# Two MLPs' first matrix: seven block products over six of eight input tiles, three tiles of h in DRAM, copies issued later

## The chip, the core and the metric

The kernel runs on one core of a Trainium2 chip. The time is device microseconds of that core for one launch; the time before is the median of three runs. The comparison asks for the same time, less or more.

## What is computed

Two groups of tokens, a prompt of 1024 and eight samples of eight, go through a trunk of two layers. Layer 0 mixes by gated linear attention, layer 1 by sliding-window attention; both have a squared-ReLU MLP from 1024 to 4096 features and back, and a per-layer input (PLE). The change touches the MLPs and what leads to them:

```python
def sq_relu_mlp(hn, w_up, w_down):
    return jnp.square(jax.nn.relu(hn @ w_up)) @ w_down
for i in range(DEPTH):                         # DEPTH = 2
    hn = rmsnorm(h, w['norm_mix'][i])
    ...                                        # y: the layer's mixer
    h = h + y
    h = h + sq_relu_mlp(rmsnorm(h, w['norm_mlp'][i]), w['w_up'][i], w['w_down'][i])
    gate = jax.nn.sigmoid(rmsnorm(h, w['norm_ple'][i]) @ w['w_ple_gate'][i])
    h = h + gate * (p[i] @ w['w_ple'][i])
```

All of it is fp32: w_up is 1024 x 4096 and w_down 4096 x 1024 in each layer.

## The kernel before

The 1088 tokens lie transposed, features on the partitions: the residual h is eight tiles of 128 x 1088 fp32, and a matmul streams token columns past a 128 x 128 block of weights. Every fp32 product is three matmuls of a narrower fp32 kind (`mm3`, L186 to L191): an operand is split into a rounded part `hi` and a rest `lo`, and hi.hi, hi.lo and lo.hi are added up in PSUM. A **k-unit** below is one input tile against one 128-wide block of weights and half of a pair's columns: two chunks of 272 columns, three matmuls each, so six matmuls.

Weights come from DRAM as fp32. SP issues the loads (`load`, L76) in one fixed order, the one in which the program asks for them; a DMA that must wait holds up those behind it on SP. `wfill` (L116 to L144) prepares weights three entries ahead of their use: a raw tile (two buffers), ScalarE's cast to `whi` (L142), VectorE's difference to `wlo` (L143), five buffers each. The order on each engine is set by a tile scheduler when the program is built and is fixed from then on.

An MLP (`mlp`, L817) has eight blocks fb of 512 hidden features. A block is two calls of `up_pair` (L741), each making two 128-wide hidden tiles, and then eight **down tiles**: for each of the eight tiles of h, 36 matmuls of 362 or 364 columns, and VectorE adds the result to h (L841). The last block begins the next norm behind each of its tiles and opens the pools of the PLE (`ple_open`, L851), whose input `praw` is loaded, cast (L218) and split (L219) there, twice, through one buffer.

`up_pair` views weights and tokens as 2 x 2 blocks. Over four of the eight input tiles (0, 1 and 2, 3) it makes seven block products in place of eight, with sums of weights (L161 to L166, VectorE, in `up_weights`) and half sums of activations (`half_sums`, L714) made once a layer while `out_proj` (L681) ends; the other four tiles (entries C1 and C2) go the plain way. The outputs pass through VectorE (L770, L771, L774, L782) and ScalarE (L772, L773, copies L778). PSUM has eight banks, `mm` 3, `gx` 3, `gs` 2; `up_pair` and the down tiles use mm and gx alone, and a down tile takes three, mm, gx, mm.

In layer 0, `bias_copies` (L929) issues at the start of each block a copy inside DRAM of 384 KB (`ed`), which later stages of layer 1 need; in the last block also two of 960 KB each that shift the caches (out_kcs, out_vcs). POOL moves pieces of `ed` on (L953, L955) when all copies are there.

## Time and profile before

| | |
|---|---|
| median of three runs | 2709.98 us (2709.81 to 2712.33) |
| the profiled execution, whole | 2710.06 us |
| its span in the trace | 2708.3 us |
| granted TensorE clock, mean | 0.997 |
| PE busy | 2665.8 us, 98 %, 18369 matmuls |
| VectorE (DVE) busy | 1735.6 us, 64 % |
| ScalarE (ACT) busy | 1162.2 us, 43 % |
| GpSimd (POOL) busy | 127.5 us, 5 % |

The profile shows one execution. Its own time is 1.8 us over its span; every position below is in us from the span's start. The stages of the two MLPs repeat eight times each, so their lengths can be read off in one block each: in layer 0 an up stage begins at 749.86 and its down stage at 796.80, in layer 1 at 2010.39 and 2055.55. The first up stages begin at 558.16 and 1822.72, the last down stages at 1270.76 and 2520.50.

### The profile page before, as it was taken

The numbers are of one execution on the slowest core, as the hardware profiler recorded it, in microseconds if no ns is written. First come the engines' busy times: TensorE is split into PE (matmuls) and PEld (weight loads), VectorE is DVE, ScalarE is ACT, GpSimd is POOL, SyncE is SP. The second block draws the span as 40 slices with busy tenths as digits, with TensorE's granted clock in tenths as the row PEclk, the third lists the DMA queues.
The fourth block names the chain that finished last, engine by engine and source line by source line (L and its number), as shares of the span: only waits on it lengthen the run. The fifth ranks groups of instructions, "written<-read, shape, count | busy, mean of one in ns | idle before, by whom it ended". The sixth has DMA issues, their size and how long they took to land.

```text
span 2708.3 us, 46678 instructions
## 1 busy us (share of the span) xinstructions
PE 2665.8 (98%) x18369; PEld 2595.9 (96%) x18369; DVE 1735.6 (64%) x4377; ACT 1162.2 (43%) x2694; POOL 127.5 (5%) x154
## 2 busy tenths in 40 slices
PE   9999999999999999999999999999999999999997
PEld 8999999999999999999999988799999999999997
DVE  5787786584565466456755677676655655565787
ACT  5565576351232233124524666554322322332565
POOL 0000000001001000010000333200000000000000
PEclk9999999999999999999999999999999999999999
DMA  3121112311111121122122111222111111111252
GB/s 126 40 65 42 57 46 72 104 47 47 57 55 35 57 62 36 46 88 63 52 81 64 50 37 49 63 69 59 40 43 48 55 34 50 51 46 34 67 179 98
DMA packets 92801, 163.56 MB, mean 60 GB/s; under 512 B 11558, under 2 KB 30650, under 8 KB 92549
## 3 DMA queue, kind: packets, MB, share of 16 engines
q1 hardware_dynamic: 89637, 155.20, 18.6%
q10 hardware_dynamic: 1152, 4.46, 0.5%
q8 instruction: 144, 2.36, 0.4%
q0 software_dynamic: 1792, 0.92, 0.2%
q14 instruction: 76, 0.62, 0.1%
HBM read 145.95 MB, written 19.98 MB: 61 GB/s over the span
## 4 chain that ended last, share of the span: by engine, by line
PE 94%; DVE 3%; ACT 2%; issue 0%; DMA 0%; POOL 0%; DVEq 0%; SPq 0%; ACTq 0%; POOLq 0%
PE mm L191 20%; PE mm L189 20%; PE mm L190 20%; PE gx L191 8%; PE gx L190 8%; PE gx L189 8%; PE gx L549 2%; PE gx L1162 1%; PE gx L1148 1%; PE gx L578 1%; PE gx L573 1%; PE gs L1131 1%; PE gx L580 0%; PE gs L257 0%; PE gs L1132 0%
## 5 line engine op out<-in xcount | busy, mean ns | idle before, releaser
L189 PE MATMUL mm<-G,whi 128*128 128x362 f32 (+2 forms) x3160 | 1014.2, 322 | 15.7 <-ACT whi L142 9.5
L191 PE MATMUL mm<-G,wlo 128*128 128x362 f32 (+2 forms) x3160 | 1012.6, 320 | 0.8
L190 PE MATMUL mm<-G,whi 128*128 128x362 f32 (+2 forms) x3160 | 1010.8, 320 | 0.0
L189 PEld LDWEIGHTS mm<-G,whi 128*128 128x128 f32 x3160 | 594.8, 188 | 23.6 <-ACT whi L142 11.8
L191 PEld LDWEIGHTS mm<-G,wlo 128*128 128x128 f32 x3160 | 594.4, 188 | 5.4 <-DVE wlo L143 2.8
L190 PEld LDWEIGHTS mm<-G,whi 128*128 128x128 f32 x3160 | 594.9, 188 | 3.5 <-issue 1.7
L191 PE MATMUL gx<-G,wlo 128*128 128x272 f32 (+2 forms) x1304 | 397.5, 305 | 0.0
L190 PE MATMUL gx<-G,whi 128*128 128x272 f32 (+2 forms) x1304 | 397.4, 305 | 0.0
L189 PE MATMUL gx<-G,whi 128*128 128x272 f32 (+2 forms) x1304 | 397.1, 305 | 0.0
L142 ACT CAST whi<-raw 128x512 fp32r<-128x512 f32 (+1 forms) x304 | 187.2, 618 | 398.8 <-PE mm L190 318.2
L841 DVE TENSOR_TENSOR H<-H,mm 128x364 f32<-128x364 f32 (+1 forms) x256 | 135.9, 531 | 227.0 <-PE mm L191 226.3
L143 DVE TENSOR_TENSOR wlo<-raw,whi 128x512 fp32r<-128x512 f32 (+1 forms) x304 | 208.5, 687 | 73.5 <-ACT whi L142 72.7
L190 PEld LDWEIGHTS gx<-G,whi 128*128 128x128 f32 x1304 | 246.1, 189 | 0.1
L191 PEld LDWEIGHTS gx<-G,wlo 128*128 128x128 f32 x1304 | 246.1, 189 | 0.0
L189 PEld LDWEIGHTS gx<-G,whi 128*128 128x128 f32 x1304 | 245.9, 189 | 0.1
L772 ACT ACTIVATE tmp<-tmp 128x272 f32<-128x272 f32 x256 | 109.5, 432 | 270.5 <-DVE tmp L771 269.1
L841 DVE TENSOR_TENSOR H<-H,gx 128x362 f32<-128x362 f32 x128 | 68.0, 531 | 137.3 <-PE gx L191 137.2
L774 DVE TENSOR_TENSOR G<-tmp,G 128x272 fp32r<-128x272 f32 x256 | 111.5, 439 | 59.5 <-ACT G L773 58.7
L142 ACT CAST whi<-sum 128x512 fp32r<-128x512 f32 x64 | 39.5, 618 | 178.0 <-PE mm L190 150.3
L771 DVE SCALAR_TENSOR_TENSOR tmp<-tmp,rb 128x272 f32<-128x272 f32 x256 | 110.9, 437 | 3.7
L251 ACT ACTIVATE tmp<-H 128x362 f32<-128x362 f32 (+1 forms) x126 | 63.6, 507 | 114.0 <-DVE H L678 57.3
L773 ACT CAST G<-tmp 128x272 fp32r<-128x272 f32 x256 | 106.2, 419 | 5.2
(295 smaller groups left out, 4057.1 us busy)
## 6 DMA issues: line engine op xcount, KB each, us to landing
raw<-in_w_down SPq DMA_DIRECT2D x128, 256.0 KB
a<-in_w_up SPq DMA_DIRECT2D x64, 256.0 KB
raw<-in_w_up SPq DMA_DIRECT2D x64, 256.0 KB
G<-in_w_gate SPq DMA_DIRECT2D x24, 512.0 KB
raw<-in_w_o SPq DMA_DIRECT2D x32, 256.0 KB
raw<-in_w_q SPq DMA_DIRECT2D x24, 256.0 KB
x<-in_xT ACTq DMA_DIRECT2D x8, 544.0 KB
hd<-H SPq DMA_DIRECT2D x8, 544.0 KB
```

The costliest lines, as they stand in the source:

```text
L142: nc.scalar.copy(hi[:, s], raw[:, s])
L143: nc.vector.tensor_tensor(lo[:, s], raw[:, s], hi[:, s].bitcast(F32), op=ALU.subtract)
L189: mm(out, lhsT=w[0], rhs=x[0], start=first, stop=False)
L190: mm(out, lhsT=w[0], rhs=x[1], start=False, stop=False)
L191: mm(out, lhsT=w[1], rhs=x[0], start=False, stop=last)
L251: nc.scalar.activation(sq[:, :cn], h[:, s], AF.Square)
L549: nc.tensor.matmul(pp[:m, l * hw:(l + 1) * hw], lhsT=E[:, l, :m], rhs=ev[:, :, 1, :], start=True, stop=True)
L771: nc.vector.scalar_tensor_tensor(t, t, 0.0, rb[:, s], op0=ALU.max, op1=ALU.mult)
L772: nc.scalar.activation(t, t, AF.Square)
L773: nc.scalar.copy(u[:, 0, s], t)
L774: nc.vector.tensor_tensor(u[:, 1, s], t, u[:, 0, s].bitcast(F32), op=ALU.subtract)
L841: nc.vector.tensor_tensor(h[:, s], h[:, s], ps, op=ALU.add)
```

## The change

- `up_pair` makes seven products over six of the eight input tiles (three and three), and two tiles go the plain way: 7 x 3 + 4 x 2 = 29 k-units a pair where there were 7 x 2 + 4 x 4 = 30. PE's order holds 192 fewer rows for matmuls, six in each of 32 pairs. The product of C1 with the second half of the tokens is begun early in the two `gs` banks and finished there by S4.
- w_up lies in DRAM as one row of 1024 for each hidden tile. Its first 768 columns (A11 and A12, or A21 and A22; 384 KB) go into tiles `a1` and `a2`, one buffer each, loaded ahead at entries A22 and C2 of the pair before; the last 256 columns are C1 or C2 (128 KB). A pair has nine weight entries (seven of 384 columns, two of 256) where it had five of 512 and one of 256. The four sums of a pair are 384 wide instead of 256, in one buffer.
- To make room, the tiles 0, 1 and 2 of h live in DRAM (`hx`). Each is stored by POOL after its update, and SP loads the next of the three into the same tile `stage`; the down tiles of a block go in the order 0, 3, 4, 1, 5, 6, 2, 7. The last block keeps the order 0 to 7 and loads tiles 1 and 2 into two tiles of its own. POOL and SP issue 48 more DMAs each.
- `half_sums` is called three times in each layer (after tiles 4, 5, 6) where it was called twice.
- `bias_copies` is called after a block's up pairs instead of before them.
- The scratch for dynamic DMAs is 2048 instead of 4096.

```diff
     def up_weights(self, which, src):
-        nc, st = self.nc, self.st
-        q = 2 * P
-        if which == "A1":
-            raw = self.a1 = st.tile([P, 512], F32, tag="a1", name=self.uid("a1"), bufs=1)
-            self.load(raw, src)
-            return raw
-        if which == "A22":
-            return self.a2[:, q:]
+
+        nc, st, q = self.nc, self.st, KS * P
+
+        def ahead(key, tag):
+            nxt = next((e for e in self.wplan[len(self.wtiles) + 1:] if e[3] == key), None)
+            if nxt is not None and nxt[0][1] == self.upl:
+                begin(nxt, tag)
+
+        def begin(entry, tag):
+            t = st.tile([P, 2 * q], F32, tag=tag, name=self.uid(tag), bufs=1)
+            self.load(t, entry[1])
+            self.up_raw[tag] = t
+        entry = self.wplan[len(self.wtiles)]
+        if which == "A11":
+            if entry[0][1] != self.upl:
+                self.upl, self.up_raw = entry[0][1], {}
+                begin(entry, "a1")
+            self.a1 = self.up_raw["a1"]
+        elif which == "S2" and "a2" not in self.up_raw:
+            begin(entry, "a2")
         a1 = self.a1
-        s = st.tile([P, 512], F32, tag="sum", name=self.uid("sum"), bufs=2)
-        if which == "S2S1":
-            a2 = self.a2 = st.tile([P, 512], F32, tag="a2", name=self.uid("a2"), bufs=1)
-            self.load(a2, src)
+        if which == "S2":
+            a2 = self.a2 = self.up_raw["a2"]
+            s = self.sums = st.tile([P, 2 * q], F32, tag="sum", name=self.uid("sum"), bufs=1)
             nc.vector.tensor_tensor(s[:, q:], a2[:, :q], a2[:, q:], op=ALU.add)
             nc.vector.tensor_tensor(s[:, :q], s[:, q:], a1[:, :q], op=ALU.subtract)
-            self.s2 = s
-        else:
-            nc.vector.tensor_tensor(s[:, q:], a1[:, :q], self.a2[:, :q], op=ALU.subtract)
-            nc.vector.tensor_tensor(s[:, :q], a1[:, q:], self.s2[:, :q], op=ALU.subtract)
-        return s
+        elif which == "S3":
+            nc.vector.tensor_tensor(self.sums[:, q:], a1[:, :q], self.a2[:, :q], op=ALU.subtract)
+        elif which == "S4":
+            nc.vector.tensor_tensor(self.sums[:, :q], a1[:, q:], self.sums[:, :q], op=ALU.subtract)
+        elif which == "A22":
+            ahead("A11", "a1")
+            return self.a2[:, q:]
+        elif which == "C2":
+            ahead("S2", "a2")
+        if which[0] == "A":
+            return a1[:, :q] if which == "A11" else a1[:, q:]
+        return self.sums[:, :q] if which in ("S2", "S4") else self.sums[:, q:]
...
-            self.split(d, h, self.gain(gain, j), CH if j >= 6 else ((0, HT if j < 2 else T),))
+            self.split(d, h, self.gain(gain, j), CH if j >= 6 else ((0, HT if j < KS else T),))
             self.hg.append(d)
-            if j in (4, 6):
-                self.half_sums(j // 2 - 2, gain)
+            if j < KS:
+                nc.gpsimd.dma_start(self.hx[j], h)
+            if 4 <= j < 4 + KS:
+                self.half_sums(j - 4, gain)
+        self.stage = self.single()
         self.norm_end()
...
-        a1, s21 = nxt("A1"), nxt("S2S1")
+        prod = lambda ps, which, x, *a: add(ps, take(nxt(which), KS), x, *a)
+        conv = lambda ps, w, off, *a: add(ps, take(w, KT - 2 * KS), lambda k: (xs[k + 2 * KS], off), *a)
         ps = bank()
-        add(ps, take(a1, 0), lambda k: (xs[k], 0), True)
+        prod(ps, "A11", lambda k: (xs[k], 0), True)
         copies(p1, ps)
         ps = bank()
-        add(ps, take(s21, 0), lambda k: (tx[k][1], 0), True)
+        prod(ps, "S2", lambda k: (tx[k][1], 0), True)
         sums(x, p1, ps)
         ps = bank()
-        add(ps, take(a1, 2), lambda k: (xs[k + 2], 0), True, False)
-        c1 = nxt("C1")
-        add(ps, take(c1, 0, 4), lambda k: (xs[k + 4], 0))
+        prod(ps, "A12", lambda k: (xs[k + KS], 0), True, False)
+        w = nxt("C1")
+        conv(ps, w, 0)
         out(0, 0, p1, ps)
+        pc = bank(("gs", "gs"))
+        conv(pc, w, HT, True, False)
         ps = bank()
-        add(ps, take(s21, 2), lambda k: (tx[k][0], 0), True)
+        prod(ps, "S1", lambda k: (tx[k][0], 0), True)
         copies(p5, ps)
-        s43 = nxt("S4S3")
         ps = bank()
-        add(ps, take(s43, 2), lambda k: (tx[k][2], 0), True)
+        prod(ps, "S3", lambda k: (tx[k][2], 0), True)
         sums(u3, x, ps)
         sums(x, x, p5)
         sums(p5, p5, u3)
+        prod(pc, "S4", lambda k: (xs[k + KS], HT))
+        out(0, 1, x, pc)
         ps = bank()
-        add(ps, take(s43, 0), lambda k: (xs[k + 2], HT), True, False)
-        add(ps, take(c1, 0, 4), lambda k: (xs[k + 4], HT))
-        out(0, 1, x, ps)
-        ps = bank()
-        add(ps, take(nxt("A22"), 0), lambda k: (tx[k][3], 0), True, False)
-        c2 = nxt("C2")
-        add(ps, take(c2, 0, 4), lambda k: (xs[k + 4], 0))
+        prod(ps, "A22", lambda k: (tx[k][3], 0), True, False)
+        w = nxt("C2")
+        conv(ps, w, 0)
         out(1, 0, u3, ps)
         ps = bank()
-        add(ps, take(c2, 0, 4), lambda k: (xs[k + 4], HT), True)
+        conv(ps, w, HT, True)
         out(1, 1, p5, ps)
...
         pt = ("mm", "gx")
+        self.load(self.stage, self.hx[0])
         for fb in range(FB):
+            last = fb == FB - 1
             us = []
-            if layer == 0:
-                self.bias_copies(fb)
             for f in range(0, FT, 2):
                 us += [self.double(utag) for _ in range(2)]
                 self.up_pair(layer, fb * FT + f, xs, us[f:])
+            if layer == 0:
+                self.bias_copies(fb)
             if fb == FB - 1:
                 self.norm_begin()
                 self.stx.close()
                 self.ple_open(layer)
-            for j in range(KT):
+            if last:
+                self.h[0] = self.stage
+                for j in range(1, KS):
+                    self.h[j] = self.pl.tile([P, T], F32, name=self.uid("h"))
+                    self.load(self.h[j], self.hx[j])
+            for j in range(KT) if last else ORD:
                 ws = self.wtile([("down", layer, fb, j)])
-                h = self.h[j]
+                h = self.stage if j < KS and not last else self.h[j]
                 def evac(c0, cn, ps):
                     s = slice(c0, c0 + cn)
                     nc.vector.tensor_tensor(h[:, s], h[:, s], ps, op=ALU.add)
                 self.gemm(ws, us, evac, kouter=(j == 0), tags=pt)
-                if fb == FB - 1:
+                if last:
                     self.norm_add(h)
                     d = self.double(tags[j // 4])
                     self.split(d, h, self.gain(gain, j), CH if j >= 6 else ((0, T),))
                     self.hg.append(d)
+                elif j < KS:
+                    nc.gpsimd.dma_start(self.hx[j], h)
+                    self.load(h, self.hx[(j + 1) % KS])
         self.norm_end()
...
                     src = I["w_up"][layer]
-                    w.append((("up", layer, f, "A1"), src[2 * f], 512, "A1"))
-                    w.append((("up", layer, f, "S2S1"), src[2 * f + 2], 512, "S2S1"))
-                    w.append((("up", layer, f, "C1"), src[2 * f + 1], 512, None))
-                    w.append((("up", layer, f, "S4S3"), None, 512, "S4S3"))
-                    w.append((("up", layer, f, "A22"), None, 256, "A22"))
-                    w.append((("up", layer, f, "C2"), src[2 * f + 3], 512, None))
-                for j in range(KT):
+                    st, cv = slice(0, 2 * KS * P), slice(2 * KS * P, D)
+                    for which in ("A11", "S2", "A12", "C1", "S1", "S3", "S4", "A22", "C2"):
+                        t = src[f + (which in ("S2", "C2"))]
+                        if which[0] == "C":
+                            w.append((("up", layer, f, which), t[:, cv], D - 2 * KS * P, which if which == "C2" else None))
+                        else:
+                            w.append((("up", layer, f, which), t[:, st], KS * P, which))
+                for j in ORD if fb < FB - 1 else range(KT):
                     w.append((("down", layer, fb, j), I["w_down"][layer, fb * KT + j], 512, None))
```

**What moves in the order.** Three places, each as the order of the engine's instructions has it, without times; numbers in names are buffers.

ScalarE, in the first up pair of a block of layer 0, before: L778 and L772, L773 belong to the outputs, L142 casts weights. The pair's last cast from a loaded tile, C2's, is the one of `raw_7735`; A22's, of `a_7577`, stands ahead.

```order
L142 CAST whi_7685<-a_7577 128x256
L778 COPY pq_6695<-mm_7689 128x272
L778 COPY pq_6695<-gx_7690 128x272
...
L773 CAST G_7676<-tmp_7771 128x272
L772 ACTIVATE tmp_7857<-tmp_7857 128x272
L773 CAST G_7676<-tmp_7857 128x272
L772 ACTIVATE tmp_7863<-tmp_7863 128x272
L773 CAST G_7676<-tmp_7863 128x272
L142 CAST whi_7737<-raw_7735 128x512
L142 CAST whi_7795<-a_7793 128x512
```

The same place now (L148 casts weights, L805 and L806 are the outputs, L811 the copies); A22's cast is that of `a_7195`, C2's that of `raw_7886`.

```order
L148 CAST whi_7814<-sum_7635 128x384
L148 CAST whi_7860<-a_7195 128x384
L805 ACTIVATE tmp_7830<-tmp_7830 128x272
L806 CAST G_7732<-tmp_7830 128x272
L805 ACTIVATE tmp_7836<-tmp_7836 128x272
L148 CAST whi_7890<-raw_7886 128x256
L806 CAST G_7732<-tmp_7836 128x272
L811 COPY pq_6735<-mm_7856 128x272
L148 CAST whi_7918<-a_7858 128x384
```

C2's cast stood behind the outputs of both earlier results; now it stands between the two output pairs of the first.

SP, at the last block of layer 0, before: the copies, then the last weights of the up stage and what follows to the down stage.

```order
L78 DMA raw_13489<-in_w_up 128x512
L78 DMA ed<-ed_5522 256x1x384
L78 DMA out_kcs<-in_kpast 8x2x15360
L78 DMA out_vcs<-in_vpast 8x2x15360
L78 DMA raw_13599<-in_w_up 128x512
...
L78 DMA raw_13953<-in_w_down 128x512
L78 DMA raw_14031<-in_w_down 128x512
L78 DMA raw_14049<-in_w_down 128x512
L78 DMA praw_14134<-in_pT 128x1088
L78 DMA praw_14139<-in_pT 128x1088
L78 DMA raw_14144<-in_w_down 128x512
```

Now:

```order
L81 DMA raw_14173<-in_w_down 128x512
L81 DMA raw_14211<-in_w_down 128x512
L81 DMA raw_14235<-in_w_down 128x512
L81 DMA ed<-ed_5522 256x1x384
L81 DMA out_kcs<-in_kpast 8x2x15360
L81 DMA out_vcs<-in_vpast 8x2x15360
L81 DMA praw_14299<-in_pT 128x1088
L81 DMA praw_14304<-in_pT 128x1088
L81 DMA h_14309<-hx_5743 128x1088
L81 DMA h_14311<-hx_5743 128x1088
L81 DMA raw_14313<-in_w_down 128x512
```

The three copies moved behind the third down weights; the PLE's input, tiles 1 and 2 of h and the fourth down weights now follow them.

SP, from a middle block of layer 1 into the next, now (before, the loads of weights alone stood here):

```order
L81 DMA raw_22102<-in_w_down 128x512
L81 DMA H_20470<-hx_19679 128x1088
L81 DMA raw_22152<-in_w_down 128x512
L81 DMA raw_22200<-in_w_down 128x512
L81 DMA raw_22248<-in_w_down 128x512
L81 DMA H_20470<-hx_19679 128x1088
L81 DMA raw_22298<-in_w_down 128x512
L81 DMA H_20470<-hx_19679 128x1088
L81 DMA raw_22493<-in_w_up 128x256
L81 DMA a_22615<-in_w_up 128x768
```

The three loads of h, each of which waits for POOL's store of the tile before it, are new; the last stands right ahead of the next pair's C1 (`raw_22493`).

## Rows read from the trace of the kernel before

**Rows 1.** The page's first and fourth part: busy us, share of the span and instructions of each engine; the chain that ended last, by engine.

```profile
PE 2665.8 (98%) x18369; PEld 2595.9 (96%) x18369; DVE 1735.6 (64%) x4377; ACT 1162.2 (43%) x2694; POOL 127.5 (5%) x154
...
PE 94%; DVE 3%; ACT 2%; issue 0%; DMA 0%; POOL 0%; DVEq 0%; SPq 0%; ACTq 0%; POOLq 0%
```

**Rows 2.** Windows of stages: up and down of a middle block of layer 0, the up stage of a middle block of layer 1, the first up stages of layer 1 and of layer 0. Columns: the stretch, its us, busy us (and instructions) of PE, PEld, DVE, ACT, POOL, granted clock, DMA engines' busy share, GB/s.

```profile
749.86:796.80 46.94, 45.69 (x362) 45.26 (x361) 32.16 (x77) 20.34 (x49) 0.00 (x0) 1.00 0.19 52
796.80:844.67 47.87, 47.87 (x290) 47.87 (x289) 20.30 (x40) 6.26 (x12) 6.86 (x12) 1.00 0.17 49
2010.39:2055.55 45.16, 45.16 (x362) 45.16 (x361) 32.09 (x76) 20.55 (x48) 0.00 (x0) 1.00 0.19 54
1822.72:1869.50 46.78, 46.78 (x366) 46.12 (x365) 40.20 (x96) 26.90 (x65) 0.00 (x0) 1.00 0.18 52
558.16:607.10 48.94, 47.34 (x365) 46.12 (x364) 41.44 (x97) 27.53 (x67) 0.00 (x0) 1.00 0.17 49
```

**Rows 3.** The waits of PE: the line that waited, what it waited for, us in total, times, the longest.

```profile
PE mm L189 <- ACT whi L142: 9.5, 8, 1.3
```

**Rows 4.** The timeline in layer 0's block of rows 2: start, us, engine, line, operation, and in brackets the engine's idle time before and what ended it. The cast is that of C2.

```profile
767.08 0.61 ACT L142 CAST whi<-raw 128x512 fp32r<-128x512 f32 x1
...
767.75 0.40 PE L189 MATMUL mm<-G,whi 128*128 128x272 f32 x1 [1.16 <-ACT whi L142]
```

**Rows 5.** The timeline of ScalarE at the same place in layer 1.

```profile
2014.99 0.62 ACT L142 CAST whi<-raw 128x512 fp32r<-128x512 f32 x1 [2.48 <-PE gx L190]
```

**Rows 6.** VectorE's instructions by line and shape: count, busy us and mean ns of one, idle before and what ended it. L143 is the lo-split, L161 one of the sums, L774 an output.

```profile
L143 DVE TENSOR_TENSOR wlo<-raw,whi 128x512 fp32r<-128x512 f32 x300 | 205.7, 687 | 73.5 <-ACT whi L142 72.7
L774 DVE TENSOR_TENSOR G<-tmp,G 128x272 fp32r<-128x272 f32 x256 | 111.5, 439 | 59.5 <-ACT G L773 58.7
...
L161 DVE TENSOR_TENSOR sum<-a 128x256 f32<-128x256 f32 x32 | 13.5, 423 | 24.6 <-DMA a<-in_w_up 24.2
...
L143 DVE TENSOR_TENSOR wlo<-a,whi 128x256 fp32r<-128x256 f32 x32 | 13.4, 418 | 0.1
```

**Rows 7.** The timeline of SP and of POOL at one load of a 544 KB tile (x from hd) and its consumer. SPq rows are issues, their us the issuing.

```profile
1735.54 0.33 SPq L78 DMA_DIRECT2D x<-hd  x1
...
1738.97 2.55 POOL L702 TENSOR_TENSOR H<-H,x 128x1088 f32<-128x1088 f32 x1 [1.50 <-DMA x<-hd]
```

**Rows 8.** DMA issues of POOL: count, KB each, median us from issue to landing.

```profile
bs<-rows POOLq DMA_DIRECT2D x2, 256.0 KB, 3.0
```

**Rows 9.** The timeline of SP in the last block of layer 0 around the copies (this is still in the seventh block's down stage).

```profile
1189.68 0.33 SPq L78 DMA_DIRECT2D raw<-in_w_up  x1
1190.05 0.60 SPq L78 DMA_DIRECT2D ed<-ed  x1
1190.69 2.35 SPq L78 DMA_DIRECT2D out_kcs<-in_kpast  x1
1193.08 0.68 SPq L78 DMA_DIRECT2D out_vcs<-in_vpast  x1
...
1201.36 0.33 SPq L78 DMA_DIRECT2D a<-in_w_up  x1
```

**Rows 10.** The timeline of POOL there: the first move of a piece of ed.

```profile
1200.80 0.58 POOL L953 DMA_DIRECT2D bs<-ed  x1 [182.80 <-DMA ed<-ed]
```

**Rows 11.** Windows there, columns as in rows 2; the last two are the DMA engines' busy share and GB/s.

```profile
1197.00:1201.00 4.00, 4.00 (x26) 4.00 (x25) 1.38 (x3) 0.62 (x1) 0.20 (x1) 1.00 0.68 281
1201.00:1205.00 4.00, 4.00 (x26) 4.00 (x25) 1.40 (x3) 0.00 (x0) 3.54 (x7) 1.00 0.53 202
1205.00:1208.00 3.00, 3.00 (x20) 3.00 (x19) 1.18 (x2) 0.62 (x1) 0.84 (x2) 1.00 0.31 107
...
1209.00:1210.00 1.00, 1.00 (x8) 1.00 (x7) 0.00 (x0) 0.00 (x0) 0.30 (x1) 1.00 0.14 46
1210.00:1211.00 1.00, 1.00 (x8) 1.00 (x7) 0.53 (x1) 0.00 (x0) 1.00 (x3) 1.00 0.08 21
```

**Rows 12.** The timelines of SP, ScalarE and VectorE around the end of layer 0's last up stage (1270.76).

```profile
1259.60 0.33 SPq L78 DMA_DIRECT2D raw<-in_w_down  x1
1264.94 6.11 SPq L78 DMA_DIRECT2D praw<-in_pT  x2
...
1268.26 1.11 ACT L218 CAST p<-praw 128x1088 fp32r<-128x1088 f32 x1
...
1269.40 1.29 DVE L219 TENSOR_TENSOR p<-praw,p 128x1088 fp32r<-128x1088 f32 x1 [0.30 <-ACT p L218]
```

**Rows 13.** The window of layer 0's last down stage, columns as in rows 2.

```profile
1270.76:1318.70 47.94, 47.94 (x291) 47.94 (x290) 40.37 (x71) 28.41 (x49) 0.00 (x0) 1.00 0.23 73
```

**Rows 14.** Windows in layer 1's attention, before, in and after a stretch of lowered clock; columns as in rows 2, the third from the end is the granted clock.

```profile
1695.00:1700.00 5.00, 3.98 (x34) 2.89 (x32) 3.83 (x20) 3.23 (x13) 0.00 (x0) 1.00 0.01 3
1700.00:1705.00 5.00, 3.79 (x26) 2.85 (x27) 4.07 (x16) 2.74 (x10) 2.03 (x2) 0.68 0.21 52
1705.00:1710.00 5.00, 5.00 (x40) 4.29 (x39) 2.42 (x11) 2.57 (x11) 0.00 (x0) 0.64 0.01 2
```

**Rows 15.** Windows ahead of the first up stages of layer 0 and of layer 1, columns as in rows 2.

```profile
538.00:549.00 11.00, 11.00 (x68) 11.00 (x67) 5.79 (x13) 3.48 (x7) 0.00 (x0) 1.00 0.36 103
549.00:558.16 9.16, 9.16 (x57) 9.04 (x56) 9.03 (x21) 7.72 (x15) 0.00 (x0) 1.00 0.16 58
...
1807.00:1822.72 15.72, 15.72 (x96) 15.60 (x95) 13.13 (x27) 10.97 (x22) 0.00 (x0) 1.00 0.22 70
```

More of the change, by code (lines that the diff above doesn't have):

```diff
@@ L22 @@
 KT = D // P
+KS = 3
 SEQ = 1024
@@ L38 @@
 WMAX = 544
+ORD = (0, 3, 4, 1, 5, 6, 2, 7)
 HT, CT = T // 2, T // 4
@@ L62, in __init__ @@
         self.n = 0
+        self.upl = None
         self.psbufs = {"mm": 3, "gs": 2, "gx": 3}
@@ L120, in wfill @@
             nc = self.nc
-            if isinstance(gains, str):
+            if isinstance(gains, str) and gains != "C2":
                 raw, gains = self.up_weights(gains, src), None
@@ L131, in wfill @@
                 self.load(raw[:, :width], src)
+                if gains == "C2":
+                    self.up_weights(gains, src)
+                    gains = None
             hi = self.wp.tile([P, WMAX], F32R, tag="hi", name=self.uid("whi"), bufs=5)
@@ L685, in out_proj @@
         self.tx = []
+        self.hx = self.dram.tile([KS, P, T], F32, name=self.uid("hx"))
         self.norm_begin()
@@ L717, in half_sums @@
         nc = self.nc
-        h1, h2, g1, g2 = self.h[i], self.h[i + 2], self.gain(gain, i), self.gain(gain, i + 2)
-        tiles = [self.hg[i][:, :, HT:]] + [self.st.tile([P, 2, HT], F32R, name=self.uid("tx")) for _ in range(3)]
+        h1, h2, g1, g2 = self.h[i], self.h[i + KS], self.gain(gain, i), self.gain(gain, i + KS)
+        tiles = [self.hg[i][:, :, HT:]]
+        for n in range(3):
+            if i == KS - 1 and n:
+                tiles.append(self.act.tile([P, 2, HT], F32R, tag="H", name=self.uid("tx"), bufs=8))
+            else:
+                tiles.append(self.st.tile([P, 2, HT], F32R, name=self.uid("tx")))
         self.tx.append(tiles)
@@ L745, in up_pair, with bank, take @@
         tx = self.tx
-        def bank():
-            return [self.ps(tag)[:, :CT] for tag in ("mm", "gx")]
-        def take(key, i, count=2):
-            hi, lo = key
-            return [(hi[:, k * P:(k + 1) * P], lo[:, k * P:(k + 1) * P]) for k in range(i, i + count)]
+        def bank(tags=("mm", "gx")):
+            return [self.ps(tag)[:, :CT] for tag in tags]
+        def take(w, count):
+            return [tuple(t[:, k * P:(k + 1) * P] for t in w) for k in range(count)]
         def add(pss, ws, x, first=False, stop=True):
@@ L1236, in rest @@
                     src = I["w_up"][layer]
[L1237 to L1243 removed]
+                    st, cv = slice(0, 2 * KS * P), slice(2 * KS * P, D)
[3 more added lines that the diff above has]
+                            w.append((("up", layer, f, which), t[:, cv], D - 2 * KS * P, which if which == "C2" else None))
+                        else:
+                            w.append((("up", layer, f, which), t[:, st], KS * P, which))
+                for j in ORD if fb < FB - 1 else range(KT):
                     w.append((("down", layer, fb, j), I["w_down"][layer, fb * KT + j], 512, None))
@@ L1357, in _layout @@
     a["w_o0"] = tiles(w_out_a[0])
-    a["w_up"] = np.stack([tiles(w) for w in w_up])
+    a["w_up"] = w_up.reshape(2, KT, P, FB * FT, P).transpose(0, 3, 2, 1, 4).reshape(2, FB * FT, P, D)
     a["w_down"] = w_down.reshape(2, FB, FT, P, KT, P).transpose(0, 1, 4, 3, 2, 5).reshape(2, FB * KT, P, 512)
@@ L1381 @@
     from concourse.bass_utils import run_bass_kernel_spmd as _run
-    nc = _bacc.Bacc("TRN2", target_bir_lowering=False, num_devices=1, dynamic_dma_scratch_size=4096)
+    nc = _bacc.Bacc("TRN2", target_bir_lowering=False, num_devices=1, dynamic_dma_scratch_size=2048)
     arrays = _layout(**{k: np.asarray(v) for k, v in inputs.items()})
```

## The prediction

> **What bounds the kernel now.** The page's first part comes first: TensorE is busy for 98 % of the span, VectorE for 64 %, ScalarE for 43 %, and the chain that ended last runs through PE for 94 % [rows 1]. A removed matmul is therefore worth its issue step wherever PE doesn't wait, and anything that newly makes PE wait costs its whole length. The windows by stage say where PE waits already [rows 2]: in layer 1 an up stage takes 45.16 us, all of it PE; in layer 0 the same 360 matmuls take 46.94 us, PE busy for 45.69. A down stage takes 47.87 and is full. The waits of PE name the cause: eight waits for ScalarE's weight cast, 9.5 us [rows 3], one in each of layer 0's eight blocks. The timeline shows one [rows 4]: the cast of the raw C2 weights stands behind four output pairs L772/L773 on ScalarE, ends at 767.69, and PE resumes at 767.75 after 1.16 us idle. VectorE is the next engine: 32 of 45 us in an up stage [rows 2], and 9.03 of the 9.16 us ahead of layer 0's first one [rows 15].
>
> The profiled execution took 2710.06 us, 0.08 over the median of the three runs; the sum is made against it, so it needs no correction. A difference under 0.2 % (5.4 us) is taken as none.
>
> **The change part by part.**
>
> *Matmuls.* A pair goes from 30 to 29 k-units of 6 matmuls: 32 x 6 = 192 fewer, all 272 columns wide. The step of one is 45.16/362 = 0.125 us [rows 2]. PE is full there, so all of it counts: **-24.0 us**.
>
> *Layer 0's stall.* The bias copies now follow the up pairs. The order on ScalarE shows C2's cast ahead of the output pairs in layer 0 too, and the copy no longer stands between the loads. In layer 1, where no copy is issued, the raw cast ran at 2014.99, well clear of the outputs, and PE never waited [rows 5]. If layer 0's up stages come to layer 1's length, that is 8 x (46.94 - 45.16) = **-14.3 us**; the lower end is the waits alone, 9.5 [rows 3].
>
> *Splits and sums.* A pair had five 512-wide lo-splits (687 ns) and one of 256 (418): 3.85 us of VectorE; now seven of 384 and two of 256 [rows 6]. No 384 row exists; midway between the rows is 0.55, so 4.72. The four sums go from 4 x 0.42 to about 4 x 0.55. That is +1.4 us of VectorE per pair, +0.9 of ScalarE. A stage of two pairs then has 35 us of VectorE in 43.6 (80 %, from 71 %). Weights are prepared three entries ahead, and one entry lasts 2.25 us of PE (18 steps), so a late split has some 6 us of cover. I take **0**; the bounds are 0 and +0.7 us per pair (+22), the latter if half of the added VectorE time reached PE.
>
> *Three tiles of h in DRAM.* Each is updated, stored by POOL, and the next one is loaded by SP into the same tile. A load of the same 544 KB took 3.4 us from issue (1735.54) to its consumer (1738.97) [rows 7]. For a store POOL has only the 256 KB row, 3.0 us to landing [rows 8]; I take 3.9, bounds 3.0 and 7 (twice the load). A trip is then 7.3 us. Such tiles stand at places 1, 4 and 7 of eight: from the last update of place 1 (6.0 + 0.5 us) to the first update of place 4 (18 + 2) there are over 12 us. So mid-stage **0**. Tighter is what stands behind it on SP: after the third tile's store, the load back, then C1's load for the next pair. That tile's last update ends at 42.9 of the down stage's 47.9, its store lands at 46.8, and C1's weights, behind the load back, some 4 us later, at about +3 of the up stage. They are needed, cast and split, after three products, 3 x 2.25 = +6.8: 3 us to spare. **0**, and a rival below.
>
> *The last block of layer 0.* The copies move from before the up pairs to before the last down tiles; in that block 384 + 2 x 960 KB go out. In the profile SP issues them from 1190.05 to 1193.76 [rows 9]. POOL, which waits for the small copy, starts at 1200.80, 10.7 us after its issue [rows 10]. The DMA windows show 0.68 and 0.53 of the engines' time taken until 1205, 0.31 until 1208, and then still 46 and 21 GB/s, 67 KB, from 1209 to 1211: the rest of the 256 KB load issued at 1201.36, held up behind the copies [rows 9, 11]. So loads issued behind them are whole only 20 us after. There they fell in a down stage and an up pair whose weights were already there. The order on SP now puts two praw loads, two h loads and the fourth down weights behind them. Before, praw's first load took 3.3 us to its cast (1264.94 to 1268.26), then came cast 1.11 and split 1.29 [rows 12]; the second praw, which needs the same buffer, takes as much again. Call E the end of the last up stage, 1270.76 before. The last down weights ahead of praw were issued at E-11.2 and praw, once its buffer was free, at E-5.8; I put the copies between them, at E-8. Then the first praw is whole at about E+12.5 and split at E+15, the second is whole at E+18.4 and split at E+21. The update of the second down tile stands behind that split on VectorE, and its h lands at about that time too (544 KB at the 281 GB/s of the windows is 2 us more). PE has six banks and takes three a tile, so it stops in the third tile, at E+16, instead of running on as it did [rows 13], until about E+22.5; the fourth down weights, last in the queue, add 1 to 2. Then a lowered clock may follow a wait: after PE was busy only 3.98 of 5 us its granted clock stood at 0.68 and 0.64 of the upper of its two levels for ten us, 3.4 us lost [rows 14]. I take **+9**, bounds 5 and 12. In layer 1 no copies exist: 0.
>
> By the Trainium skill ("DMA: Bandwidth & Descriptors", "Why a DMA increments its semaphore by 16 and not by 1") a transfer is spread over as many DMA engines as divide its slowest dimension: 2 for the small copy, 8 for the big ones. By that rule half the engines stay free, yet a 128-partition load uses all sixteen and is whole only when the busy ones are through; the rows agree, with 0.31 to 0.68 busy and 67 KB late. Were the queue shared fairly instead, the term would be near 0 and the sum 2675.
>
> *Into the up stages.* A third pair of half sums adds sixteen 272-wide operations a layer, 16 x 0.44 = 7 us of VectorE [rows 6]. From 538 to 549 VectorE is idle for 5.2 us, from 549 to 558 for 0.1; before layer 1's up stage, of 15.7 us, for 2.6 [rows 15]. So 2 to 4 us a layer can show. Part of it is needed only from the second product on. **+3**, bounds 0 and 6.
>
> *Sum:* 2710.06 - 24.0 - 14.3 + 9 + 3 = 2683.8, so **2684 us**. With the terms at their ends: 2677 to 2695.
>
> **Rivals.**
> *The copies are hidden after all* (15 %). Half the DMA engines are idle while they run [rows 11]; if praw and h slip past, the +9 is gone: 2675, or 2672 without the transition's 3. Against it: the late load, and POOL's 10.7 us.
>
> *VectorE becomes the bound of the up stages* (14 %). For it: 80 % busy, with a chain sum, split, product in every entry. Against it: layer 1's first up stage has VectorE at 40.20 of 46.78 us, 86 %, and PE busy throughout [rows 2]. At 0.3 to 0.7 us a pair, +10 to +22: 2694 to 2706.
>
> *SP is blocked by the store* (10 %; this one ends slower). The third load back waits for POOL's store, and C1's load can't pass it. Seven block boundaries in each of two layers see it, so each us beyond the 3 us of cover costs 14 us. A saving of 26 is eaten at 1.9 us more: the store would have to take 3.9 + 3 + 1.9 = 8.8 us. At 10 us the time is about 2727. For it: no row shows a 544 KB store by POOL at all, and copies landed as late as 10.7 us. Against it: the 3.0 us row, and DMA engines 12 to 19 % busy in these stages [rows 2].
>
> *It doesn't do what it says* (1 %). Seven products on six tiles save one k-unit in thirty only; the matmul count in the order confirms the 192, so at worst both gains are swallowed, about 2710.
>
> **How the numbers follow.** My forecast has 60 %, its own range 2677 to 2695. The hidden copies add 2671 to 2676 below and the lighter half of the VectorE case a little above: 2671 to 2698 holds about 81 %. Faster by over 0.2 %: 60 + 15 + 11 of the 14 = 0.86. Slower: 8 of the 10, and 1 of the 14, 0.09. Within: 0.05.
>
> **What would show it.** PE with 192 fewer matmuls; both layers' block periods near 91.5 us; the eight waits on the cast gone. In the last block of layer 0 a wait of PE 16 us into the down stage, with the update of h and a cast behind DMA, and ScalarE's praw cast late. I am wrong if PE waits at each block's start for C1, if the middle up stages are longer than 43.8 us, or if PE never stops in that last down stage.

## The result and the profile after

The changed kernel takes 2690.76 us (median of four runs, 2690.75 to 2691.45) against 2711.15 for the kernel before in four: a ratio of 0.9927, 95 % interval 0.9916 to 0.9939, so about 0.7 % faster; the medians differ by 20.4 us. The time lies in the forecast's own range, 7 us above its figure. The page after, its engines:

```profile
PE 2642.5 (98%) x18177; PEld 2572.5 (96%) x18177; DVE 1779.0 (66%) x4505; ACT 1190.5 (44%) x2814; POOL 154.5 (6%) x202
```

PE has 192 matmuls fewer than in [rows 1] and 23.3 us less to do; the span fell by 19.3. Windows of stages after, columns as in [rows 2]: up and down of a middle block of layer 0, then of layer 1, then layer 0's last down stage in two pieces.

```profile
745.90:789.52 43.62, 43.62 (x349) 43.62 (x349) 34.73 (x83) 20.93 (x52) 0.00 (x0) 1.00 0.28 88
1999.32:2042.92 43.60, 43.60 (x349) 43.60 (x349) 35.16 (x83) 21.56 (x53) 0.00 (x0) 1.00 0.27 83
789.52:838.49 48.97, 48.08 (x291) 47.77 (x290) 19.95 (x40) 6.93 (x15) 1.62 (x3) 1.00 0.25 86
2042.92:2090.73 47.81, 47.81 (x290) 47.81 (x289) 19.68 (x40) 6.66 (x14) 1.59 (x3) 1.00 0.24 85
...
1252.74:1268.70 15.96, 15.96 (x98) 15.77 (x96) 7.01 (x13) 6.37 (x12) 6.93 (x12) 1.00 0.30 113
1268.70:1278.00 9.30, 2.78 (x10) 2.67 (x10) 4.46 (x8) 3.78 (x6) 0.00 (x0) 0.66 0.64 236
```

The up stages are alike in both layers and full, 43.6 us, where they were 46.9 and 45.2 [rows 2]. The down stages are not: layer 0's middle ones take 49.0 us, layer 1's 47.8, the old length [rows 2]. In layer 0's last down stage PE runs full for 16 us and then nearly stands. The waits of PE (line, what it waited for, total us, times, longest) name both:

```profile
PE mm L213 <- DVE h L881: 6.5, 1, 6.5
PE mm L215 <- DVE wlo L149: 6.3, 7, 0.9
```

The old eight waits on ScalarE's cast [rows 3] are gone. In their place stand seven short waits on a lo-split and one long one on an update of h.

**The seven short waits.** SP, ScalarE, VectorE and PE in the block whose down stage starts at 789.52 (start, us, engine, line, operation, in brackets the idle time before and what ended it):

```profile
781.55 0.60 SPq L81 DMA_DIRECT2D ed<-ed  x1
783.42 0.81 SPq L81 DMA_DIRECT2D raw<-in_w_down  x1
...
792.39 0.61 ACT L148 CAST whi<-raw 128x512 fp32r<-128x512 f32 x1
...
803.65 0.53 DVE L881 TENSOR_TENSOR H<-H,mm 128x364 f32<-128x364 f32 x1 [1.46 <-PE mm L215]
805.63 0.53 DVE L881 TENSOR_TENSOR H<-H,gx 128x362 f32<-128x362 f32 x1 [1.45 <-PE gx L215]
807.63 0.53 DVE L881 TENSOR_TENSOR H<-H,mm 128x362 f32<-128x362 f32 x1 [1.46 <-PE mm L215]
808.08 1.29 DVE L149 TENSOR_TENSOR wlo<-raw,whi 128x512 fp32r<-128x512 f32 x2
...
808.82 0.44 PE L215 MATMUL mm<-G,wlo 128*128 128x364 f32 x1 [0.89 <-DVE wlo L149]
```

The fourth down weights are loaded behind the copy, and their cast is over at 793.0. Their lo-split runs only at 808.08, although VectorE is idle for over a microsecond three times in between: it stands behind the ninth update of h, which waits for PE, and PE then waits for the split. Its operands were there; the fixed order held it back. The order of VectorE in a middle block of layer 0, at the end of the third tile, and in layer 1, where the split stands thirteen operations of the outputs ahead of the first update (in the block whose down stage starts at 2042.92 it runs at 2040.63, the first update at 2048.11):

```
layer 0:  L881 TENSOR_TENSOR H_6174<-H_6174,mm_11449 128x362
          L149 TENSOR_TENSOR wlo_11320<-raw_11317,whi_11319 128x512     the fourth
          L149 TENSOR_TENSOR wlo_11370<-raw_11367,whi_11369 128x512
layer 1:  L149 TENSOR_TENSOR wlo_22105<-raw_22102,whi_22104 128x512     the fourth
          ...
          L881 TENSOR_TENSOR H_20470<-H_20470,mm_22108 128x364          the first update
```

**The long wait.** SP, ScalarE, VectorE and PE at layer 0's last down stage, which starts at 1252.74:

```profile
1244.78 0.59 SPq L81 DMA_DIRECT2D ed<-ed  x1
1245.42 2.15 SPq L81 DMA_DIRECT2D out_kcs<-in_kpast  x1
1247.62 0.67 SPq L81 DMA_DIRECT2D out_vcs<-in_vpast  x1
1249.54 19.47 SPq L81 DMA_DIRECT2D praw<-in_pT  x2
...
1266.22 1.11 ACT L242 CAST p<-praw 128x1088 fp32r<-128x1088 f32 x1 [5.15 <-DMA praw<-in_pT]
1272.42 1.10 ACT L242 CAST p<-praw 128x1088 fp32r<-128x1088 f32 x1 [5.09 <-DMA praw<-in_pT]
...
1273.55 1.29 DVE L243 TENSOR_TENSOR p<-praw,p 128x1088 fp32r<-128x1088 f32 x1 [4.89 <-ACT p L242]
1274.75 0.53 DVE L881 TENSOR_TENSOR h<-h,mm 128x364 f32<-128x364 f32 x1
...
1275.33 0.67 PE L213 MATMUL mm<-G,whi 128*128 128x362 f32 x1 [6.52 <-DVE h L881]
```

The first praw needs 16.7 us from issue to cast, 3.3 before [rows 12]; the second follows, its split stands ahead of the second tile's update on VectorE, and PE gets a bank 22.6 us into the stage. The granted clock from 1268.7 to 1278 is 0.66. While the first praw is still on its way the DMA engines are busy for only 0.19 of the time (the last column but one):

```profile
1260.00:1264.00 4.00, 4.00 (x26) 4.00 (x25) 1.35 (x1) 1.08 (x1) 0.56 (x1) 1.00 0.19 63
```

Last, the rows that the forecast had no pattern for: POOL's stores and SP's loads of hx (median us to landing), the issue of C1's load behind the load of h with its cast, and VectorE's 384-wide splits.

```profile
hx<-H POOLq DMA_DIRECT2D x48, 544.0 KB, 3.0
H<-hx SPq DMA_DIRECT2D x44, 544.0 KB, 3.7
...
836.95 0.38 SPq L81 DMA_DIRECT2D raw<-in_w_up  x1
...
840.51 0.41 ACT L148 CAST whi<-raw 128x256 fp32r<-128x256 f32 x1 [0.31 <-DMA raw<-in_w_up]
...
L149 DVE TENSOR_TENSOR wlo<-sum,whi 128x384 fp32r<-128x384 f32 x128 | 69.4, 553 | 8.2 <-ACT whi L148 8.0
```

### The profile page after: what moved, and what is told of

The parts are those of the page before. It is cut to its first block, busy times and chain, and to the rows that moved or that the text cites. A ratio compares the mean times of both kernels' runs of the same rounds, so it can differ in the third digit from the quotient of the medians.

```text
span 2689.0 us, 46921 instructions
## 1 busy us (share of the span) xinstructions
PE 2642.5 (98%) x18177; PEld 2572.5 (96%) x18177; DVE 1779.0 (66%) x4505; ACT 1190.5 (44%) x2814; POOL 154.5 (6%) x202
## 4 chain that ended last, share of the span: by engine, by line
PE 93%; DVE 3%; ACT 1%; DMA 1%; issue 1%; POOL 0%; SPq 0%; DVEq 0%; ACTq 0%; POOLq 0%
PE mm L213 19%; PE mm L215 19%; PE mm L214 19%; PE gx L215 7%; PE gx L214 7%; PE gx L213 7%; PE gx L573 2%; PE gs L214 2%; PE gs L215 1%; PE gs L213 1%; PE gx L1205 1%; PE gx L1191 1%; DMA praw<-in_pT 1%; PE gx L602 1%; PE gx L597 1%
## 5 line engine op out<-in xcount | busy, mean ns | idle before, releaser
L213 PE MATMUL mm<-G,whi 128*128 128x362 f32 (+2 forms) x2872 | 932.7, 326 | 12.5 <-DVE h L881 6.5
L215 PE MATMUL mm<-G,wlo 128*128 128x362 f32 (+2 forms) x2872 | 931.5, 324 | 6.4 <-DVE wlo L149 6.3
L214 PE MATMUL mm<-G,whi 128*128 128x362 f32 (+2 forms) x2872 | 929.4, 324 | 0.0
L213 PEld LDWEIGHTS mm<-G,whi 128*128 128x128 f32 x2872 | 541.8, 189 | 19.3 <-DVE h L881 6.8
L214 PEld LDWEIGHTS mm<-G,whi 128*128 128x128 f32 x2872 | 542.1, 189 | 3.8 <-issue 1.7
L148 ACT CAST whi<-raw 128x512 fp32r<-128x512 f32 (+2 forms) x304 | 173.2, 572 | 517.6 <-DMA raw<-in_w_down 402.0
L215 PE MATMUL gx<-G,wlo 128*128 128x362 f32 (+2 forms) x1016 | 314.9, 310 | 0.0
L214 PE MATMUL gx<-G,whi 128*128 128x362 f32 (+2 forms) x1016 | 314.7, 310 | 0.0
L213 PE MATMUL gx<-G,whi 128*128 128x362 f32 (+2 forms) x1016 | 313.9, 309 | 0.0
L881 DVE TENSOR_TENSOR H<-H,mm 128x364 f32<-128x364 f32 x248 | 131.8, 531 | 268.0 <-PE mm L215 267.6
L149 DVE TENSOR_TENSOR wlo<-raw,whi 128x512 fp32r<-128x512 f32 (+2 forms) x304 | 190.8, 632 | 122.3 <-ACT whi L148 122.0
L213 PEld LDWEIGHTS gx<-G,whi 128*128 128x128 f32 x1016 | 192.1, 189 | 0.0
L215 PEld LDWEIGHTS gx<-G,wlo 128*128 128x128 f32 x1016 | 192.1, 189 | 0.0
L214 PEld LDWEIGHTS gx<-G,whi 128*128 128x128 f32 x1016 | 192.1, 189 | 0.0
L805 ACT ACTIVATE tmp<-tmp 128x272 f32<-128x272 f32 x256 | 109.1, 430 | 107.4 <-DVE tmp L804 106.1
L811 ACT COPY pq<-mm 128x272 f32<-128x272 f32 x64 | 24.6, 384 | 191.1 <-PE mm L215 190.9
L806 ACT CAST G<-tmp 128x272 fp32r<-128x272 f32 x256 | 105.8, 418 | 5.7
```

The costliest lines, as they stand in the source:

```text
L148: nc.scalar.copy(hi[:, s], raw[:, s])
L149: nc.vector.tensor_tensor(lo[:, s], raw[:, s], hi[:, s].bitcast(F32), op=ALU.subtract)
L213: mm(out, lhsT=w[0], rhs=x[0], start=first, stop=False)
L214: mm(out, lhsT=w[0], rhs=x[1], start=False, stop=False)
L215: mm(out, lhsT=w[1], rhs=x[0], start=False, stop=last)
L805: nc.scalar.activation(t, t, AF.Square)
```

## The experiments

Theory 1: both new waits of layer 0 come from the place of the copies inside DRAM, the short ones through the order of VectorE, the long one through the DMA engines. Its rivals: hx's traffic, the loads of h, VectorE's load, or SP behind the stores. Medians of four runs (ten for before_moved); the kernel before stood at 2709.2 to 2710.3 beside them.

**ed_late**: the small copy of blocks 0 to 6 goes out after the fifth down tile.

```diff
-            if layer == 0:
+            if layer == 0 and last:
                 self.bias_copies(fb)
...
+                if layer == 0 and not last and n == 4:
+                    self.bias_copies(fb)
```

> In blocks 0 to 6 of layer 0 the 384 KB copy is issued after the fifth down tile instead of ahead of the fourth down weights' load; the last block is as in the changed kernel. Theory 1 (the order: with the copy ahead of that load, the fourth weights' lo-split is put behind the ninth update of h in VectorE's order, and PE waits 0.9 us for it in each of seven blocks): the split stands ahead of the updates again, as in layer 1; layer 0's down stages fall from 49.0 to 47.85 us, seven times, and the time from 2690.8 to about 2682.7. Theory 2 (the longer down stages come from the traffic of hx, stores and loads that meet the copies): the traffic is the same, so they stay at 49.0 or the loss moves, and the time stays within 2 us of 2690.8.

Measured: 2683.93 us, ratio 0.9900 (0.9884 to 0.9917). The wait on the split is gone from the list, and a middle down stage is back at 47.81 us (787.93 to 835.74) with hx's stores and loads unchanged. Theory 1 holds, the rival with hx's traffic falls.

**caches_early**: no copy in the last block (cache_copy issues one of the two big ones).

```diff
-            if layer == 0:
+            if layer == 0 and not last:
                 self.bias_copies(fb)
...
+                if layer == 0 and n == 4:
+                    if fb in (2, 4):
+                        self.cache_copy(fb // 2 - 1)
+                    if fb == FB - 2:
+                        self.bias_copies(fb + 1)
```

> The last block of layer 0 issues no copy: its 384 KB go out in block 6 and the two of 960 KB in blocks 2 and 4, each after the fifth down tile; the other blocks are as in the changed kernel. Theory 1 (in the last block praw is held up behind the copies and with it the update of the second tile): the first praw is cast some 3.5 us after its issue instead of 16.7, the 6.5 us wait of PE goes, and that down stage falls from 56.0 to about 47.9; time about 2682.7. Theory 2 (the two loads of h in the last block, new in the change, are what is late, copies or not): the stage stays above 52 us, time 2687 or more. Where the big copies now run, a load of h or of weights behind them may be late: up to 2 us each.

Measured: 2682.94 us, 0.9901 (0.9886 to 0.9916). The wait on the update of h is gone, the seven on the split are still there. The loads of h in the last block make PE wait for nothing by themselves.

**both_moved**: both edits.

> Both of the edits before in one: every copy of layer 0 goes out after a fifth down tile, none in the last block. If the two losses are separate, as theory 1 has it, they add up: 2690.8 - 8.0 - 8.1 = about 2674.7, with layer 0's block periods at 91.5 us like layer 1's. If the one loss hides part of the other, or if the moved copies meet the loads of h, more than 2678.

Measured: 2674.38 us, 0.9866 (0.9851 to 0.9881). Both waits are gone from PE's list; the down stages of layer 0 in this kernel, a middle one and the last:

```profile
786.80:834.60 47.80, 47.80 (x291) 47.80 (x290) 19.83 (x40) 6.64 (x14) 1.67 (x3) 1.00 0.32 111
1244.20:1292.00 47.80, 47.80 (x290) 47.80 (x289) 41.34 (x73) 30.02 (x52) 0.00 (x0) 1.00 0.29 96
```

The two losses are separate and add up. This version beats both kernels: 16 us under the changed one.

**old_place**: the changed kernel, with the copies issued ahead of a block's up pairs as before.

```diff
+            if layer == 0:
+                self.bias_copies(fb)
             for f in range(0, FT, 2):
                 us += [self.double(utag) for _ in range(2)]
                 self.up_pair(layer, fb * FT + f, xs, us[f:])
-            if layer == 0:
-                self.bias_copies(fb)
```

> The changed kernel with the copies issued where they were before, ahead of a block's up pairs. The order now has C2's cast ahead of the outputs and the fourth down weights' split ahead of the updates, so by these alone layer 0 loses neither the old 1.8 us in an up stage nor the new 1.15 in a down stage: 2690.8 - 8.0 - 8.1 = 2674.7 (theory 2: the copies' place costs nothing more). Theory 1: SP issues the copy right behind the load of h that waits for the store, and C1's load behind the copy; C1 landed 5 us ahead of its need, the copy holds two DMA engines for 8 us, so PE waits 1 to 3 us at C1 in blocks 1 to 6 and some 10 to 13 us in the last block, behind the two big copies: 2690 to 2706.

Measured: 2729.51 us, 1.0067 (1.0052 to 1.0082), slower than the kernel before. The side is theory 1's, the size is not: 23 us above its range. The waits of PE, then SP and ScalarE at the start of the up stage at 756.06, and windows of it:

```profile
PE mm L213 <- ACT whi L148: 35.8, 8, 13.8
```

```profile
754.20 0.33 SPq L81 DMA_DIRECT2D H<-hx  x1
754.59 0.61 SPq L81 DMA_DIRECT2D ed<-ed  x1
755.28 2.79 SPq L81 DMA_DIRECT2D raw<-in_w_up  x1
...
765.70 0.40 ACT L148 CAST whi<-raw 128x256 fp32r<-128x256 f32 x1 [6.75 <-DMA raw<-in_w_up]
```

```profile
756.06:762.80 6.74, 6.74 (x56) 6.74 (x54) 1.41 (x3) 0.77 (x2) 0.00 (x0) 1.00 0.32 112
762.80:766.00 3.20, 0.24 (x2) 0.02 (x1) 0.00 (x0) 0.30 (x1) 0.00 (x0) 0.88 0.10 39
766.00:770.00 4.00, 3.84 (x17) 3.85 (x18) 3.60 (x9) 2.11 (x6) 0.00 (x0) 0.50 0.31 74
770.00:774.00 4.00, 4.00 (x26) 4.00 (x26) 2.30 (x7) 2.14 (x6) 0.00 (x0) 0.74 0.56 188
```

C1's weights are cast 10.4 us after the issue of their load, 3.6 in the changed kernel (836.95 to 840.51); what is new ahead of it on SP is the copy. PE stops at C1, 6.7 us into the stage, for 3.1 us in this block and 13.8 in the last; block 0, which the expectation did not count, waits too. What else it left out is the clock: 0.50 in the next four microseconds and 0.74 in the four after, 3.0 us more. A block loses 5 to 6 us, not 1 to 3, the last one 16.7.

**before_moved**: the kernel before with this one move.

```diff
-            if layer == 0:
-                self.bias_copies(fb)
             for f in range(0, FT, 2):
                 us += [self.double(utag) for _ in range(2)]
                 self.up_pair(layer, fb * FT + f, xs, us[f:])
+            if layer == 0:
+                self.bias_copies(fb)
```

> The kernel before with one edit: the copies are called after a block's up pairs. Theory 1 (moving the copies alone trades waits): C2's cast comes ahead of the outputs, 8 x 1.8 = -14.3; the fourth down weights' split falls behind the ninth update in VectorE's order, 7 x 1.15 = +8.0; in the last block praw is late behind the copies and the second tile's update stands behind its split, +8: together +1.8, 2711 to 2713, no gain. Theory 2 (in the kernel before, with all of h on the chip, the last block does not wait): 2703 to 2705. Theory 3 (the move alone is worth its saving of the old stall): 2695 to 2697.

Measured: 2717.68 us, 1.0025 (1.0016 to 1.0034): slower by 7. Its waits of PE, and windows of a middle up and down stage of layer 0:

```profile
PE mm L189 <- ACT whi L142: 9.8, 1, 9.8
PE mm L191 <- DVE wlo L143: 6.2, 7, 0.9
```

```profile
749.90:795.00 45.10, 45.10 (x361) 45.10 (x360) 31.67 (x76) 20.15 (x48) 0.00 (x0) 1.00 0.18 56
795.00:844.00 49.00, 48.11 (x290) 47.81 (x289) 20.80 (x40) 6.72 (x13) 0.00 (x0) 1.00 0.13 44
```

The trade is theory 1's: 1.8 us gained in each up stage, 1.1 lost in each down stage, seven times, for the same split. The last block loses more than the 8 expected: its down stage takes 59.9 us (1265.8 to 1325.7) for 47.9, with one wait of 9.8 us, here on a weight cast that stands behind the second praw's cast on ScalarE (1293.06 behind 1292.05).

**sums_twice**: three of a pair's four sums are written twice.

```diff
             nc.vector.tensor_tensor(s[:, q:], a2[:, :q], a2[:, q:], op=ALU.add)
+            nc.vector.tensor_tensor(s[:, q:], a2[:, :q], a2[:, q:], op=ALU.add)
             nc.vector.tensor_tensor(s[:, :q], s[:, q:], a1[:, :q], op=ALU.subtract)
+            nc.vector.tensor_tensor(s[:, :q], s[:, q:], a1[:, :q], op=ALU.subtract)
...
             nc.vector.tensor_tensor(self.sums[:, q:], a1[:, :q], self.a2[:, :q], op=ALU.subtract)
+            nc.vector.tensor_tensor(self.sums[:, q:], a1[:, :q], self.a2[:, :q], op=ALU.subtract)
```

> The changed kernel with three of a pair's four sums of weights (S1, S2, S3) written twice: 3 x 0.55 = 1.65 us more of VectorE a pair, 3.3 a stage, from 34.9 to 38.2 of 43.6 us (88 %). Theory 1 (three entries of look-ahead cover it): up stages stay at 43.65, time within 3 us of 2690.8. Theory 2 (VectorE at 80 % is close to the bound): at least half of it reaches PE, 32 x 0.8 = +26, 2717 or more.

Measured: 2692.13 us, 0.9932 (0.9917 to 0.9946), within 1.4 us of the changed kernel. An up stage of layer 0:

```profile
746.00:789.60 43.60, 43.60 (x350) 43.60 (x349) 37.39 (x90) 21.23 (x53) 0.00 (x0) 1.00 0.28 86
```

VectorE at 37.39 of 43.60 us, 86 %, and PE busy throughout: up to this load the rival with VectorE as the bound falls.

**store_twice**: each store of hx in the middle blocks is issued twice.

```diff
                 elif j < KS:
                     nc.gpsimd.dma_start(self.hx[j], h)
+                    nc.gpsimd.dma_start(self.hx[j], h)
                     self.load(h, self.hx[(j + 1) % KS])
```

> The changed kernel with every store of a tile of h to DRAM in the middle blocks issued twice, one after the other, so that the load back, and C1's load behind it on SP, come about 3 us later. Theory 1 (C1's weights land 4 to 5 us ahead of their need): nothing to see at the blocks' starts, time within 3 us of 2690.8. Theory 2 (the cover is used up): 1 to 3 us at each of 14 block starts, 2705 to 2733.

Measured: 2689.96 us, 0.9924 (0.9908 to 0.9941), no difference to the changed kernel. POOL's two stores and SP's load of C1 at the end of a block of layer 1; here the next up stage starts at 2089.7:

```profile
2084.70 0.53 POOL L889 DMA_DIRECT2D hx<-H  x1 [13.70 <-DVE H L881]
2087.91 0.53 POOL L890 DMA_DIRECT2D hx<-H  x1 [2.67 <-DMA hx<-H]
```

```profile
2091.38 0.38 SPq L81 DMA_DIRECT2D raw<-in_w_up  x1
```

C1's load is issued 1.7 us into the up stage (in the block shown of the changed kernel, 1.5 us ahead of it: 836.95 against 838.49), and PE has no wait for a cast of C1 in its list: over 3 us of cover, as forecast. Little more was left: the cast ends at 2095.9, and PE needs C1, split, 6.75 us into the stage, at 2096.4.

**wide_caches**: the big copies, written row first.

```diff
-                self.load(self.O[out][:, 0:120, :], self.I[past][:, 8:128, :])
+                self.load(self.O[out][:, 0:120, :].rearrange("b s d -> s b d"),
+                          self.I[past][:, 8:128, :].rearrange("b s d -> s b d"))
```

> The changed kernel with the two 960 KB copies written row first, 120 x 8 x 256 instead of 8 x 120 x 256, in pieces of 1 KB. Theory 1 (the big copies hold half the DMA engines for 16 us, and praw waits for those; by the Trainium skill, DMA: Bandwidth & Descriptors, Why a DMA increments its semaphore by 16 and not by 1, a slowest dimension of 120 spreads over 15 engines): the copies end some 8 us sooner, praw is whole at about 4 to 6 us into the last down stage, PE no longer waits, 2682 to 2685. Theory 2 (copies inside DRAM are bound by the memory or by their smaller pieces): they take as long as before or longer, and praw waits on all engines: 2690 or more.

Measured: 2688.22 us, 0.9917 (0.9903 to 0.9932), between the two theories: 2.5 us less than the changed kernel. PE's wait on the update of h fell from 6.5 to 3.7 us. That leaves open whether the amount copied or the engines of the small copy hold praw up.

**wide_all**: the small copies too, still at the changed kernel's place.

```diff
-        self.load(self.ed[s], self.ed1[s].unsqueeze(1).broadcast_to([2, P, 384]))
+        self.load(self.ed[s].rearrange("a p c -> p a c"),
+                  self.ed1[s].unsqueeze(0).broadcast_to([P, 2, 384]))
```

> As wide_caches, and the copies of 384 KB are written 128 x 2 x 384 instead of 2 x 128 x 384; every copy is issued where the changed kernel issues it. In wide_caches PE still waited 3.7 us and the late part of praw was the share of two DMA engines, those that the small copy holds for 8 us. The order of this kernel has the fourth down weights' split ahead of the updates in all blocks of layer 0. Theory 1 (both losses come from the few engines that the copies were spread over, one of them through the order): down stages of 47.85 us in blocks 0 to 6, praw whole about 5 us into the last down stage and no wait there: 2690.8 - 8.0 - 8.1 = 2674 to 2677. Theory 2 (the amount copied holds praw up, however spread): only the 8.0 of the middle blocks goes and half of the last block's wait stays, 2679 to 2683.

Measured: 2675.77 us, 0.9876 (0.9859 to 0.9892): theory 1. Windows of a middle down stage of layer 0 and of the copies in its last block, issued here from 1235.72, and the first praw's cast, 5.8 us into the last down stage (its start is 1243.7):

```profile
786.30:834.10 47.80, 47.80 (x291) 47.80 (x290) 21.14 (x44) 7.04 (x15) 1.60 (x3) 1.00 0.24 87
...
1241.00:1247.50 6.50, 6.50 (x46) 6.50 (x45) 4.84 (x13) 3.74 (x10) 4.66 (x8) 1.00 0.98 330
1247.50:1252.00 4.50, 4.50 (x30) 4.50 (x29) 1.36 (x2) 1.10 (x1) 2.30 (x4) 1.00 0.21 62
```

```profile
1249.50 1.10 ACT L242 CAST p<-praw 128x1088 fp32r<-128x1088 f32 x1 [2.85 <-PE mm L213]
```

The same bytes at the same place: the engines are 98 % busy for a while, 21 % after it. The load of praw is still slow, 8.9 us from issue to landing, but that is 16.6 in the changed kernel, and at 1249.4 it comes early enough for PE. The long wait is gone, and so are the short ones: the order of VectorE now has the fourth split ahead of the updates (785.51, the first update at 791.46). The last down stage's matmuls end after 47.9 us, as in both_moved; behind them PE waits 1.2 and 0.7 us for VectorE's sums of the norm, which no run follows up.

## Why the prediction was right, and where not

By its own terms, from the two profiled executions, whose spans differ by 19.3 us where 26.3 was forecast:

- *Matmuls*, -24.0: right. A layer 1 up stage fell by 1.56 us by the windows, and 12 fewer matmuls at 0.125 are 1.5.
- *Layer 0's stall*, -14.3: right in the up stages, 46.94 to 43.62, which is 1.5 for the matmuls and 1.8 for the stall. But "the copy no longer stands between the loads" was true of the up stages alone. The step that failed is in that term: it moved the copy and, in blocks 0 to 6, did not look at what stands behind it at the new place, the fourth down weights. There 1.15 us are lost in each of seven blocks: **+8.0** that the sum did not have. So layer 0's block period is 92.6 us, and the 91.5 that should have shown the forecast stands in layer 1 alone. The order of VectorE, which shows the split behind the ninth update, was there to read.
- *The last block of layer 0*, +9: +8.1, by the mechanism, the place and nearly the times given (E is the end of the last up stage, now 1252.74): copies at E-8.0 (E-8), the first praw cast at E+13.5 (whole at E+12.5), the second split over at E+22.1 (E+21), PE stopped from E+16 until E+22.6 (E+22.5). caches_early takes it away whole. The fourth down weights added nothing; the lowered clock did, 1.6 us beyond the wait of 6.5.
- *Splits, sums and hx*, 0: right. 384 columns cost 0.55 us as interpolated, VectorE has 35 of 43.6 us, a store landed in 3.0 us (3.9 taken) and a load in 3.7 (3.4). sums_twice and store_twice show the covers.
- *Into the up stages*, +3: too much. Layer 0's first up stage begins where it did (558.0, before 558.2) and falls by 0.4 us less than the others, 49.06 to 46.18; PE waits there 0.7 us for the norm's sums, before 0.3. In layer 1 nothing shows: **+0.4**.
- Not in the sum: 1.7 us in layer 1's attention, where the stretch from 1683.5 to 1738.5 took 55.0 us for 53.3. Two windows there have a granted clock of 0.66 and 0.67, as [rows 14] had two in a row; what is more lies behind them, where the last 33.5 us show 0.95 and the last 31.7 before showed 1.00. No run here says why. Another 0.9 us are lost behind layer 1's last up stage, in pieces that no run follows up.

So -24.0 - 14.4 + 8.0 + 8.1 + 0.4 + 1.7 + 0.9 = -19.3, the fall of the span. That the time lies in the range although one loss was missing is in part luck: the range is 18 us wide, none of its bounds was for a loss of this kind, and 2.6 us too much for the way into the up stages and 0.9 for the last block stood against it. A small slip in the working changes nothing: seven splits at 0.55 and two at 0.42 are 4.7 us, not 4.72.

The rule of the Trainium skill on how many DMA engines a transfer gets ("DMA: Bandwidth & Descriptors", "Why a DMA increments its semaphore by 16 and not by 1") fits the runs, which do not count engines: with the shape alone changed, the busy share of the engines rose to 0.98 (0.76 at most in the windows of the changed kernel's copies) and 2690.8 became 2675.8 us. "The copies are hidden after all" did not come about, the last block lost 8.1 us to them; "SP is blocked by the store" does not happen at this place of the copies, but old_place shows it, with the copy and not the store as the blocker: 39 us between two places of the same DMAs.

That the copies are issued later is then not worth what the stall was. In the kernel before, the move alone costs 7 us. In the changed kernel the old place costs 39: by the rows C1's load now stands behind a wait for a store and has some 4 us of cover, less than the copy takes. So the new products need the move, and the place that was chosen gives away 16 us, as both_moved shows.
